# Operand parts stored by the stages, gate sums on VectorE, merge weights split in the second group

## The chip, the cores and the metric

The kernel runs on one core of a Trainium2 chip. The metric is the device time of one execution in microseconds (us), as the median of several runs. Five engines work side by side, each in the order of its own queue: TensorE (PE; its weight loads are listed as PEld), VectorE (DVE), ScalarE (ACT), GpSimd (POOL) and SyncE (SP). SP issues all transfers (DMAs) of this kernel, in the order of its queue.

## The reference

One layer over 2048 prompt rows and 8 x 16 sample rows of 1024 channels. What matters of it:

```python
h = rms_norm(x, norm_g[l])
(a_x, a_b, a_c, a_z, g_q, g_f, g_i, g_z,
 s_q, s_k, s_v, s_z, m_a, m_b, m_c) = split_cols(h @ w_in[l])
...
o_a = a_b * y_conv * jax.nn.silu(a_z)          # branch A, gated convolution
...
o_b = o_hg * jax.nn.silu(g_z)                  # branch B, linear recurrence
...
o_c = o_sb.reshape(B, T, W_SB).astype(x.dtype) * jax.nn.silu(s_z)   # branch C, stick-breaking attention
wb = w_branch[l]
y_a = o_a @ wb[:W_CONV]
y_b = o_b @ wb[W_CONV:W_CONV + W_HG]
y_c = o_c @ wb[W_CONV + W_HG:]
m = jax.nn.sigmoid(m_a) * y_a + jax.nn.sigmoid(m_b) * y_b + jax.nn.sigmoid(m_c) * y_c
return x + m @ w_out[l], conv_new, S_new.astype(x.dtype), k, v
```

All is float32. The attention is strictly causal: query block i looks at all keys before it, so later blocks cost more.

## The kernel before, in words

**Three passes per product.** A float32 operand is split into two parts (`split`, L171): ACT copies it, rounded, into the high part, and DVE subtracts that from the source to get the low part. A product is then three matmuls (`PASS3`): high x high, high x low, low x high.

**Stages.** The 17 tiles of 128 tokens are projected in three groups (`GROUPS`: 5, 6 and 6 tiles; a group has two chunks of up to 384 tokens). In a group `run_jobs` (L1241) goes through 56 channel jobs (one weight block of 128 columns, 24 matmuls per chunk, L683) and 8 token jobs (L694, two weight pieces each). After the third group comes the merge (L1321 on): four groups of 512 to 640 tokens, each with 12 branch jobs (`bjob`, three branches x by four column pieces dp) and 4 output jobs (`ojob`).

**Background work.** Between a job's pieces a planner hands out credit: the cost of each piece times a rate lets waiting background steps be recorded there. In the second group this is the attention of the sample rows; in the third group and the merge it is the prompt attention (`attn_pair`, L285), at `RATES[2]` = 0.65 and `RATE_M` = 1.0. One step of it, for 128 queries and up to 512 keys: two matmuls for the scores z (L306, L307), two sigmoids on ACT (L310, L312), a running product on DVE (L319) and a product on DVE (L324), four transposes on PE (L291), a copy aT by ACT (L292), and, after eight such steps, 16 matmuls pv with the values (L336). In the merge `bg.drain(gi)` finishes a group's attention before its branch x = 2 is loaded.

**Weights.** `wload` (L180) takes one of three buffers w (1 MB, both parts). The first time a weight is used it is loaded into a staging buffer wst (two of them, 512 KB) and split into w, and `wkeep` (L204) writes w to memory as W; later uses load W straight into w. The projection weights are split in the first group; the merge weights (12 branch pieces, 8 output pieces) in the first group of the merge. A job's weights are loaded one job ahead.

**Branch outputs.** The three branches write their outputs to OX in memory as plain float32. The merge loads them (`load_o`, L1329) through two small buffers ost, multiplies branch C by its gate SZ there, and splits each of the four row blocks into oh and ol. `bjob` multiplies the branch's product by its gate on DVE (L1374, L1376) and sums the branches with an add on POOL (L1377; on DVE only for the last branch of the last merge group). For x = 2 the sum m is split into mh and ml, some chunks late (the list `due`), for the output jobs.

**The order.** The program is recorded in the order of the Python code, and a scheduler then places each engine's instructions by its own costs and the free buffers; what it leaves is a fixed queue per engine.

## Time and profile before

| | |
|---|---|
| median of 3 runs | 2925.81 us (2923.69 to 2926.0) |
| the profiled execution, by the clock of the runs | 2919.97 us |
| its span in the trace | 2918.1 us |
| PE busy | 98% of the span, 19511 matmuls |
| DVE, ACT, POOL busy | 52%, 35%, 15% |
| DMA | 597.82 MB, 205 GB/s |

The time outside the span is 2919.97 - 2918.1 = 1.9 us. PE is busy in nearly all of the span, so time is lost or won only where PE waits; the matmuls themselves do not change. The projection of the second group runs from about 610 to 1330 us of the span, that of the third from 1350 to 2180, the merge from 2190 to the end.

### The profile page before, as it was taken

What the parts mean: (1) busy time and instruction counts of PE and PEld (TensorE: products, weight loads), DVE (VectorE), ACT (ScalarE), POOL (GpSimd) and SP (SyncE); (2) the same over time, 40 slices, a digit from 0 to 9 for tenths busy, and PEclk for the clock granted to TensorE, in tenths of its full rate; (3) what the DMA queues carried; (4) which work ended last, traced back from release to release, by engine and by line L of the source; (5) the groups of instructions that cost most, each with busy time, mean ns of one, the idle gap of its engine ahead of it and who ended that gap; (6) DMA issues with size and microseconds to landing.
All of it is one profiled execution on the core that took longest, in us unless ns stands there. A gap on an engine that the chain in (4) does not pass through costs nothing.

```text
span 2918.1 us, 51343 instructions
## 1 busy us (share of the span) xinstructions
PE 2873.3 (98%) x19511; PEld 2672.2 (92%) x19511; DVE 1530.7 (52%) x3182; ACT 1024.7 (35%) x2359; POOL 427.9 (15%) x859
## 2 busy tenths in 40 slices
PE   9999999999999999999999999999999899999999
PEld 9999999999999999999999999999988787687888
DVE  5454644641252423345434747265577876867643
ACT  4333223242222222114333443334444554444420
POOL 3200000120100000002231111101012412313210
PEclk9999999999999999999999999999999999999999
DMA  8977677767556564436764444434347776677666
GB/s 305 315 257 236 223 227 237 239 229 250 182 184 204 168 213 147 150 128 195 237 200 154 140 151 134 152 121 150 126 155 252 258 268 219 224 251 227 222 230 233
DMA packets 329224, 597.82 MB, mean 205 GB/s; under 512 B 29097, under 2 KB 231170, under 8 KB 291090
## 3 DMA queue, kind: packets, MB, share of 16 engines
q1 hardware_dynamic: 328978, 594.54, 61.8%
q8 instruction: 155, 2.54, 0.4%
q14 instruction: 91, 0.75, 0.1%
HBM read 410.62 MB, written 183.80 MB: 204 GB/s over the span
## 4 chain that ended last, share of the span: by engine, by line
PE 87%; DVE 4%; DMA 4%; issue 3%; POOL 2%; ACT 1%; SPq 0%; DVEq 0%; POOLq 0%; ACTq 0%
PE acc L683 45%; PE acc L694 13%; PE acc L1403 6%; PE acc L1368 4%; PE pv L336 4%; PE tp L291 3%; PE z L1013 2%; PE z L307 2%; PE z L306 2%; DVE pr L319 1%; PE tp L434 1%; POOL mp L1377 1%; DMA w<-W 1%; PE pv L498 1%; DMA gate<-GM 1%
## 5 line engine op out<-in xcount | busy, mean ns | idle before, releaser
L683 PE MATMUL acc<-hh,w 128*128 128x384 f32 (+1 forms) x5376 | 1465.0, 338 | 0.0
L683 PEld LDWEIGHTS acc<-hh,w 128*128 128x128 f32 x5376 | 964.3, 188 | 23.6 <-issue 17.9
L683 PE MATMUL acc<-hl,w 128*128 128x384 f32 (+1 forms) x2688 | 882.5, 328 | 0.0
L683 PEld LDWEIGHTS acc<-hl,w 128*128 128x128 f32 x2688 | 507.1, 189 | 4.9 <-issue 1.0
L694 PE MATMUL acc<-w,hh 128*128 128x256 f32 x2176 | 413.1, 286 | 1.5 <-DMA w<-W 1.2
L694 PEld LDWEIGHTS acc<-w,hh 128*128 128x128 f32 x2176 | 341.8, 188 | 4.0 <-DMA w<-W 1.5
L319 DVE TENSOR_TENSOR_SCAN pr<-snb,carry 128x513 f32<-128x513 f32 x192 | 250.6, 1306 | 117.1 <-ACT snb L310 115.6
L694 PE MATMUL acc<-w,hl 128*128 128x256 f32 x1088 | 306.8, 282 | 0.7 <-DVE hl L175 0.7
L1368 PE MATMUL acc<-oh,w 128*128 128x512 f32 (+2 forms) x960 | 295.4, 368 | 4.2 <-DMA w<-W 1.8
L292 ACT COPY aT<-tp 128x512 f32<-128x512 f32 (+2 forms) x320 | 167.6, 525 | 289.7 <-PE tp L291 289.4
L324 DVE TENSOR_TENSOR sp<-sp,pr 128x512 f32<-128x512 f32 (+2 forms) x320 | 210.3, 657 | 33.7 <-POOL sp L315 7.8
L310 ACT ACTIVATE snb<-z 128x512 f32<-128x512 f32 (+2 forms) x320 | 172.5, 539 | 129.2 <-PE z L307 120.3
L1368 PEld LDWEIGHTS acc<-oh,w 128*128 128x128 f32 x960 | 176.3, 190 | 36.9 <-DVE gate L1376 5.1
L694 PEld LDWEIGHTS acc<-w,hl 128*128 128x128 f32 x1088 | 205.1, 189 | 1.8 <-DVE hl L175 1.3
L319 DVE TENSOR_TENSOR_SCAN pr<-snb,one 128x129 f32<-128x129 f32 (+3 forms) x128 | 114.7, 896 | 163.1 <-POOL snb L315 162.9
L1403 PE MATMUL acc<-w,mh 128*128 128x256 f32 x960 | 189.1, 285 | 2.5 <-DMA w<-W 2.3
L291 PE MATMUL tp<-idf,sp 128*128 128x128 f32 x1088 | 172.0, 273 | 8.1 <-ACT aT L292 7.2
L175 DVE TENSOR_TENSOR w<-wst,w 128x1024 fp32r<-128x1024 f32 x92 | 114.9, 1249 | 121.6 <-ACT w L174 121.1
L1368 PE MATMUL acc<-ol,w 128*128 128x512 f32 (+1 forms) x480 | 174.1, 363 | 3.2 <-DVE ol L175 3.1
L312 ACT ACTIVATE sp<-z 128x512 f32<-128x512 f32 (+2 forms) x320 | 171.3, 535 | 12.6 <-DMA OX<-ot 7.5
L1403 PEld LDWEIGHTS acc<-w,mh 128*128 128x128 f32 x960 | 153.7, 188 | 10.6 <-issue 5.2
L1146 ACT ACTIVATE gm<-acc 128x384 f32<-128x384 f32 (+1 forms) x144 | 68.3, 474 | 260.8 <-PE acc L683 223.0
(296 smaller groups left out, 3730.9 us busy)
## 6 DMA issues: line engine op xcount, KB each, us to landing
w<-W SPq DMA_DIRECT2D x200, 1024.0 KB, 5.3
W<-w SPq DMA_DIRECT2D x92, 1024.0 KB, 5.0
wst<-in_w_in_dram SPq DMA_DIRECT2D x72, 512.0 KB, 6.3
GM<-gm SPq DMA_DIRECT2D x120, 192.0 KB, 2.7
Kt<-KT SPq DMA_DIRECT2D x160, 128.0 KB, 3.6
gate<-GM SPq DMA_DIRECT2D x72, 256.0 KB, 3.1
vc<-in_cache_v_dram SPq DMA_DIRECT2D x64, 256.0 KB, 3.8
kc<-in_cache_k_dram SPq DMA_DIRECT2D x64, 256.0 KB, 3.5
```

The lines of the kernel that those rows point to most:

```text
L175: return first, (eng or nc.vector).tensor_tensor(lo, src, hi.bitcast(F32), ALU.subtract)
L291: nc.tensor.transpose(tp[:, j * P:(j + 1) * P], sp[:, j * P:(j + 1) * P], idf)
L292: nc.scalar.copy(aT[:, e, 0:nb, i * P:(i + 1) * P], tp[:, :w].rearrange("p (b q) -> p b q", q=P))
L310: nc.scalar.activation(sn[:, 512 - w:512], z[:, :w], AF.Sigmoid, scale=-0.125)
L312: nc.scalar.activation(sp[:, :w], z[:, :w], AF.Sigmoid, scale=0.125)
L319: nc.vector.tensor_tensor_scan(pr[:, 512 - w:513][:, ::-1], s_in, s_in, one if diag else carry[e][i], ALU.mult, ALU.bypass)
L324: nc.vector.tensor_tensor(sp[:, :w], sp[:, :w], pr[:, 513 - w:513], ALU.mult)
L336: nc.tensor.matmul(pv[64 * e:64 * e + 64, c0:n], Vt[:, j, e], aT[:, e, j, c0:n], start=first and j == 0, stop=last and j == nb - 1, skip_g ...
L683: nc.tensor.matmul(acc[:, :n], w[0][a][:, k], hT[b][:, k, :n], start=k == 0 and i == 0, stop=k == KB - 1 and i == 2)
L694: nc.tensor.matmul(acc[:, :256], hT[b][:, k, ti * P:(ti + 1) * P], w[k // 4][a][:, k % 4], start=k == 0 and i == 0, stop=k == KB - 1 and i ...
L1368: nc.tensor.matmul(acc[:, :n], w[0][a][:, k, dd * P:(dd + 1) * P], box[x][b][:, k, sl], start=k == 0 and i == 0, stop=k == 3 and i == 2)
L1403: nc.tensor.matmul(acc[:, :256], box["l" if b else "h"][:, k, ti * P:(ti + 1) * P], w[k // 4][a][:, k % 4], start=k == 0 and i == 0, stop= ...
```

## The change

It has seven parts.

1. OX holds both parts of each branch output. The stages that make the outputs split and store them (`store_parts`): the convolution (`az`), the recurrence, the prompt attention (`store`) and the sample attention. The attention's stores also multiply by the gate SZ, which is loaded ahead.
2. `load_o` loads both parts straight into one tile o, eight DMAs and nothing else. The load for branch 0 of the next merge group is recorded ahead, in the last branch of this one; the first is recorded ahead of the first weights.
3. All sums of the branches are on DVE, and the split of m follows at once.
4. The merge weights are split and written to memory during the second group (`split_merge_weights`), one piece after the other from the ninth place on, each recorded at the second chunk of a channel job.
5. Of the loads of kept weights every fourth goes into the two wst buffers, one part each, in place of a w buffer. The last weights of the merge no longer have places of their own.
6. `RATES[2]` is 0.85 (was 0.65) and `RATE_M` 0.75 (was 1.0).
7. The two parts of the normed input, hh and hl, lie in one tile hx.

```diff
-RATES = (0.0, 0.55, 0.65)
-RATE_M = 1.0
+RATES = (0.0, 0.55, 0.85)
+RATE_M = 0.75
...
+    OX = dram.tile([3, 4, 2, P, NTOK], F32R, name="OX")
...
+    def store_parts(dst, where, x, room):
+        split(room.bitcast(F32R), x.bitcast(F32R), x)
+        for v, part in enumerate((room, x)):
+            nc.sync.dma_start(dst[v][:, where].bitcast(F32), part)
...
             if (key, n) in kept:
+                turns[0] += 1
+                if turns[0] % 4 == 0:
+                    hl = []
+                    for i in range(2):
+                        x = wp.tile([P, a, b], F32, tag="wst", name="wst", bufs=2)
+                        nc.sync.dma_start(x, kept[key, n][:, i].rearrange("p (a b) -> p a b", a=a).bitcast(F32))
+                        hl.append(x.bitcast(F32R))
+                    out.append((*hl, None))
+                    continue
+            w = wp.tile([P, 2, 1024], F32R, tag="w", name="w")
...
+            if m == m1 - 1:
+                gate.append(at.tile([P, 512], F32, tag="ot", name="ot", bufs=1))
+                nc.sync.dma_start(gate[0][:, :n], SZ[pair][:, q0:q0 + n])
...
         def store():
-            t = at.tile([P, 512], F32, tag="sp", name="ot", bufs=4)
-            nc.scalar.copy(t[:, :n], box[0][:, :n])
-            nc.sync.dma_start(OX[2, pair][:, q0:q0 + n], t[:, :n])
+            t = gate[0]
+            nc.vector.tensor_tensor(t[:, :n], box[0][:, :n], t[:, :n], ALU.mult)
+            th = at.tile([P, 512], F32, tag="oth", name="oth", bufs=1)
+            store_parts(OX[2, pair], slice(q0, q0 + n), t[:, :n], th[:, :n])
...
-            nc.sync.dma_start(OX[0, self.j][:, cols(chunk)], y)
+            store_parts(OX[0, self.j], cols(chunk), y, sg[:, :n])
...
+            oh = hs.tile([P, 2 * P], F32, tag="ktm", name="oh", bufs=1)
+            store_parts(OX[1, h], slice((first + unit[0]) * P, (first + unit[0]) * P + n), ob[:, :n], oh[:, :n])
...
+    def split_merge_weights():
+        for pieces, key in [branch_w(x, dp) for x in range(3) for dp in range(4)] + [out_w(s) for s in range(4)]:
+            for n, v in enumerate(pieces):
+                wkeep(wload([v], key, n), key, n)
+                yield
...
+        extra = split_merge_weights() if g == 1 else iter(())
         for at_, (i, ci) in enumerate(order):
+            if ci and len(jobs[i][0][0]) == 1 and at_ > 8:
+                next(extra, None)
             weights(i)
...
         def load_o(x):
-            oh = p3.tile([P, 4, GMAX], F32R, tag="oh", name="oh", bufs=2)
-            ol = p3.tile([P, 4, GMAX], F32R, tag="ol", name="ol", bufs=2)
+            o = p3.tile([P, 2, 4, GMAX], F32R, tag="o", name="o", bufs=2)
             for j in range(4):
-                st = p3.tile([P, GMAX], F32, tag="ost", name="ost", bufs=2)
-                nc.sync.dma_start(st[:, :ntok], OX[x, j][:, gcols])
-                if x == 2:
...
-                split(oh[:, j, :ntok], ol[:, j, :ntok], st[:, :ntok])
-            box[x] = (oh, ol)
+                for v in range(2):
+                    nc.sync.dma_start(o[:, v, j, :ntok].bitcast(F32), OX[x, j, v][:, gcols].bitcast(F32))
+            box[x] = (o[:, 0], o[:, 1])
...
+                if dp == 2 and x == 2 and not final:
+                    loads[gi + 1](0)
...
-                            (nc.vector if final and x == 2 else nc.gpsimd).tensor_tensor(
-                                m, m, gate[:, sl], ALU.add)
+                            nc.vector.tensor_tensor(m, m, gate[:, sl], ALU.add)
                         if x == 2:
-                            box["due"].append((box["h"][:, d, sl], box["l"][:, d, sl], m))
-                            while len(box["due"]) > (0 if final or d == 7 and chunk is pg[-1] else len(pg)):
-                                split(*box["due"].pop(0))
+                            split(box["h"][:, d, sl], box["l"][:, d, sl], m)
...
+    loads[0](0)
     ws = {0: wload(*alljobs[0][0])}
     for i, (_, compute) in enumerate(alljobs):
         if i + 1 < len(alljobs):
-            places = None
-            if i + 1 - len(alljobs) in (-3, -1):
-                places = [p3.tile([P, 4, GMAX], F32R, tag=t, name="wlast", bufs=2).rearrange("p a b -> p (a b)")
-                          [:, :2048].rearrange("p (v w) -> p v w", v=2) for t in ("oh", "ol")]
-            ws[i + 1] = wload(*alljobs[i + 1][0], places)
-        wkeep(ws[i], alljobs[i][0][1])
+            ws[i + 1] = wload(*alljobs[i + 1][0])
```

**SP's queue in the second group.** What stands in SP's queue before, at about the middle of the group's channel jobs (kc, vc and vnew are the sample attention's; w_10549 is a projection weight, loaded from its kept copy; what stands in brackets is what the row waits for, by engine or by one of eight DMA counters):

```order
L917 DMA OX_75<-y_9769 128x384 [waits DMAHW3_49,DVE_49]
L482 DMA vc_10531<-in_cache_v_dram 128x512 [waits DMAHW4_49,PE_49]
L482 DMA vc_10533<-in_cache_v_dram 128x512 [waits DMAHW5_49,PE_49]
L485 DMA vnew_6986<-VV_74 16x512 [waits DMAHW6_49,PE_49]
L1147 DMA GM_77<-gm_10348 128x384 [waits DMAHW7_49,Activation_49]
L1092 DMA OX_75<-ob_10340 128x256 [waits DMAHW0_49,DVE_49]
L189 DMA w_10549<-W31_3251 128x2048 [waits DMAHW1_49,PE_49]
```

And in the changed kernel, where two merge weight pieces are staged (wst_9683, wst_9782), written (W77, W78), and two projection weights follow (w_9743, w_9823):

```order
L211 DMA wst_9683<-in_w_branch_dram 128x4x256 [waits PE_49]
L211 DMA wst_9782<-in_w_branch_dram 128x4x256 [waits DMAHW1_49,PE_49]
L506 DMA vc_10117<-in_cache_v_dram 128x512 [waits DMAHW2_49,PE_49]
L208 DMA w_9743<-W23_2455 128x2048 [waits DMAHW3_49]
L227 DMA W77_9687<-w_9682 128x2048 [waits DMAHW4_49,DVE_49]
L227 DMA W78_9786<-w_9781 128x2048 [waits DMAHW5_49,DVE_49]
L208 DMA w_9823<-W24_2571 128x2048 [waits DMAHW6_49,DMAHW4_49]
L211 DMA wst_9902<-in_w_branch_dram 128x4x256 [waits DMAHW7_49,DMAHW0_49]
```

Before, a weight load waits for PE alone, beside the counter that it will count on itself. Now staging loads and writes stand among the weight loads: wst_9683 waits for PE, W77 for DVE, and w_9823 also for the counter DMAHW4, on which W77 counts, since it takes the buffer that W77 is written from.

**PE at the same place of the changed kernel** (acc<-hx,w is a channel job; L522 and L476 belong to the sample attention, L1040 to the recurrence; just ahead of these rows the job ends that holds wst_9630, the weight part whose buffer wst_9782 takes):

```order
L522 MATMUL pv_9715<-vc_9895,at__9889 32x128 x3
L1040 MATMUL z_9942<-WR_9931,WL_9930 128x128 [waits DVE_49,PE_49]
L476 MATMUL z_9945<-kt_9770,qz_7006 32x384 [waits PE_49]
L476 MATMUL z_9945<-kt_9770,qz_7006 32x384 x3
L1040 MATMUL z_9989<-WR_9974,WL_9973 128x128 [waits DVE_49,PE_49]
L1040 MATMUL z_10004<-WR_9993,WL_9992 128x128 [waits DVE_49,PE_49,Activation_49]
L710 MATMUL acc_9825<-hx_6801,w_9743 128x384 [waits DMAHW3_49]
L710 MATMUL acc_9825<-hx_6801,w_9743 128x384 x23
L710 MATMUL acc_9908<-hx_6980,w_9743 128x384 x24
L710 MATMUL acc_9982<-hx_6801,w_9823 128x384 [waits DMAHW6_49,Activation_49]
```

Between the last matmul of the job that frees wst_9630 and the first one with w_9823 there are now 48 matmuls with w_9743 and 31 small ones, the last ten of them shown here.

**ACT's queue in the merge.** Before, where branch C of the first merge group is loaded (snb and sp are the sigmoids of the attention):

```order
L292 COPY aT_25230<-tp_25630 128x3x128 [waits PE_49]
L310 ACTIVATE snb1_15007<-z_25646 128x512 [waits DVE_49,PE_49]
L312 ACTIVATE sp_25650<-z_25646 128x512
L174 CAST oh_25704<-ost_25706 128x640 [waits DVE_49]
L292 COPY aT_25230<-tp_25663 128x4x128 [waits PE_49]
L310 ACTIVATE snb2_15009<-z_25678 128x512 [waits PE_49,Activation_49]
L312 ACTIVATE sp_25682<-z_25678 128x512 [waits Pool_49]
L174 CAST w_25863<-wst_25864 128x1024 [waits DMAHW3_49,DMAHW0_49,PE_49]
L174 CAST oh_25704<-ost_25713 128x640 [waits DVE_49]
L292 COPY aT_25558<-tp_25758 128x4x128 [waits PE_49,Activation_49]
```

And now, in the same merge group, where the split of m begins:

```order
L311 COPY aT_26806<-tp_27057 128x4x128 [waits PE_49]
L175 CAST mh_26995<-mp_26142 128x384 [waits DMAHW4_49,DMAHW2_49,DMAHW5_49,DMAHW1_49,DMAHW6_49,DMAHW0_49,DVE_49]
L175 CAST mh_26995<-mp_26142 128x256 [waits DVE_49]
L333 ACTIVATE snb2_15328<-z_27076 128x512 [waits PE_49]
L335 ACTIVATE sp_27080<-z_27076 128x512
L175 CAST mh_26995<-mp_26142 128x384 [waits DVE_49]
L311 COPY aT_26806<-tp_27108 128x4x128 [waits PE_49]
```

The copies oh and w are gone from ACT's queue here; the copies mh, which now wait for DVE, are what is left between the attention's own instructions.

51 lines of the change are left out of this document (25 added, 26 removed).

## The prediction

> **What bounds the kernel now.** I read the stages first, then who ends PE's waits in each. The view of busy time by stretches, for the projection of the second group, that of the third, and the merge (after the length: busy us and instructions of each engine, then clock, DMA share, GB/s):
>
> ```profile
> core 0: us, PE busy (x) PEld busy (x) DVE busy (x) ACT busy (x) POOL busy (x), PEclk, DMA share, GB/s
> 610.00:1330.00 720.00, 718.33 (x5355) 698.16 (x5354) 248.49 (x728) 176.63 (x474) 42.98 (x84) 1.00 0.55 182
> 1350.00:2180.00 830.00, 828.15 (x5374) 776.32 (x5373) 459.85 (x1001) 326.99 (x817) 140.97 (x335) 1.00 0.49 157
> 2190.00:2918.00 728.00, 699.17 (x4295) 583.88 (x4295) 489.93 (x635) 299.85 (x585) 172.15 (x264) 1.00 0.72 239
> ```
>
> PE is the bound throughout. It is idle for 720 - 718.33 = 1.7 us in the second group and 1.9 us in the third: nothing is to be won there, only to be lost. The merge has 728 - 699.17 = 28.8 us of idle PE. What ended PE's waits in the merge, first on the matmuls, then on the weight loads, which wait earlier and so count more (us in total, times, longest):
>
> ```profile
> PE pv L336 <- ACT aT L292: 7.5, 5, 2.7
> PE tp L291 <- ACT aT L292: 7.2, 6, 3.3
> PE acc L1368 <- DVE ol L175: 3.1, 2, 1.9
> PE z L306 <- ACT sp L312: 2.4, 4, 1.4
> PE acc L1368 <- ACT oh L174: 1.6, 2, 1.5
> ```
>
> ```profile
> PEld pv L336 <- ACT aT L292: 13.2, 8, 3.6
> PEld tp L291 <- ACT aT L292: 9.0, 6, 3.5
> PEld acc L1368 <- DVE gate L1376: 5.1, 7, 2.0
> PEld acc L1368 <- DVE ol L175: 4.9, 4, 2.3
> PEld z L306 <- ACT sp L312: 3.6, 4, 1.6
> PEld acc L1368 <- ACT oh L174: 3.2, 3, 1.9
> PEld acc L1403 <- DVE pr L319: 1.8, 1, 1.8
> ```
>
> ACT is the one that is late, and yet it is busy for 300 of 728 us. It stands still with work behind it. Three rows of the timeline in the merge show how (start, length, in brackets the idle time ahead):
>
> ```profile
> 2479.67 0.62 ACT L174 CAST oh<-ost 128x512 fp32r<-128x512 f32 x1 [7.44 <-DVE ost L1338]
> 2480.20 0.58 ACT L292 COPY aT<-tp 128x512 f32<-128x512 f32 x1
> 2683.26 0.62 ACT L174 CAST mh<-mp 128x512 fp32r<-128x512 f32 x1 [4.17 <-POOL mp L1377]
> ```
>
> The copy oh heads ACT's queue and waits 7.44 us for a loaded and multiplied branch output. The attention's copy aT is behind it and PE behind that. At 2683 the same is done by mh, which waits for POOL's add.
>
> **The change, part by part.** *The merge.* The loads of both parts take oh, its DVE half ol and the product with SZ out of the merge, and weight splits too; POOL's adds go to DVE. So the waits for aT and sp lose their cause, in all 7.5 + 7.2 + 2.4 = 17.1 us by the matmuls, 13.2 + 9.0 + 3.6 = 25.8 us by the weight loads. The copies mh stay and now wait for DVE; they fall in one branch of three, so I leave 5 us of waits: of the middle, 21.5, I count 16 as won. The waits for oh and ol (4.7 to 8.1 us) go as well, but the first load of the merge takes their place. It reads 8 x 320 KB = 2.6 MB, and its buffers come free only when the projection's do, some 4 us of PE work (as the order of PE has it) ahead of the first branch matmul. The nearest rows are the load of one part before and the highest rates of the merge's slices:
>
> ```profile
> ost<-OX SPq DMA_DIRECT2D x12, 320.0 KB, 4.3
> GB/s 230 267 309 271 219 276 230 238 300 211 287 252 219 242 233 218 261 215 214 220 242 234 260 228 202 302 184 234 250 223 224 187 238 195 205 295 321 325 220 73
> ```
>
> At 309 to 325 GB/s it takes some 8.3 us and the first landing adds about 1; the last row block is needed 5.5 us after the issue (4, and 9 matmuls). That is a stall of about 4 us where 6.4 stood (the middle of 4.7 and 8.1): -2. Later loads have 14 us or more of PE work ahead of them and are hidden; without that cover each would cost this much again. DVE's own late rows (gate 5.1, pr 1.8) I take to improve by 2, with DVE's load: it loses 48 ol (41.9 us), 17 weight splits (23.1), 16 products (11.6) and the attention that moves out, and gains POOL's 72 adds, at the length of the 8 that DVE made already:
>
> ```profile
> L175 DVE TENSOR_TENSOR ol<-ost,oh 128x512 fp32r<-128x512 f32 (+1 forms) x48 | 41.9, 877 | 13.7 <-ACT oh L174 13.6
> L175 DVE TENSOR_TENSOR w<-wst,w 128x1024 fp32r<-128x1024 f32 x17 | 23.1, 1359 | 7.1 <-ACT w L174 7.1
> L1338 DVE TENSOR_TENSOR ost<-ost,szt 128x512 f32<-128x512 f32 (+1 forms) x16 | 11.6, 726 | 26.4 <-DMA szt<-SZ 26.3
> L1377 DVE TENSOR_TENSOR mp<-mp,gate 128x512 f32<-128x512 f32 x8 | 6.0, 755 | 0.2
> ```
>
> ```profile
> L1377 POOL TENSOR_TENSOR mp<-mp,gate 128x512 f32<-128x512 f32 (+1 forms) x72 | 108.3, 1508 | 144.7 <-DVE gate L1376 132.0 <-issue 12.2 <-DMA gate<-GM 0.3
> ```
>
> The adds cost 72 x 0.755 = 54 us on DVE against 76.6 removed; hidden, as long as DVE stays under PE. Sum for the merge -16 - 2 - 2 = **-20**; ends: -33 (25.8 and 8.1 and 5.1 all gone, 4 and 2 kept) and -12 (17.1, of which 5 stay, and no other gain).
>
> *The second group, where the merge weights are now split.* In each pair a staging buffer comes free when a job ends, wst is loaded, ACT and DVE split it, W is written, and only the landing of that write frees the buffer of a following projection weight, which is then loaded. SP issues in order, so the other weight loads of that place stand behind the waiting W too. The rows for this chain (loads and writes: KB, median us to landing; first the whole run, then the merge, then the second group):
>
> ```profile
> W<-w SPq DMA_DIRECT2D x92, 1024.0 KB, 5.0
> ```
>
> ```profile
> w<-W SPq DMA_DIRECT2D x56, 1024.0 KB, 6.2
> W<-w SPq DMA_DIRECT2D x18, 1024.0 KB, 5.9
> wst<-in_w_branch_dram SPq DMA_DIRECT2D x9, 512.0 KB, 6.4
> wst<-in_w_out_dram SPq DMA_DIRECT2D x8, 512.0 KB, 7.3
> ```
>
> ```profile
> w<-W SPq DMA_DIRECT2D x57, 1024.0 KB, 5.5
> xt<-in_x_prompt_dram SPq DMA_DIRECT2D x1, 512.0 KB, 4.8
> ```
>
> ```profile
> L174 ACT CAST w<-wst 128x1024 fp32r<-128x1024 f32 x17 | 17.9, 1054 | 13.2 <-DMA wst<-in_w_branch_dram 9.1 <-DMA Vt<-VV 2.5 <-PE acc L1403 1.3
> ```
>
> From the release to the landed weight: 6.4 + 1.05 + 1.36 + 5.0 + 5.5 = 19.3 us; with the merge's landings 6.4 + 2.4 + 5.9 + 6.2 = 20.9; I take 19.6, nearer the first, whose rows come from more transfers and from this group. The PE work that covers it, at the place shown in the order: 48 matmuls of 384 columns and 31 small ones, by these rows of the chain of waits:
>
> ```profile
> 816.12 4.22 PE acc L683 x24
> ```
>
> ```profile
> 2121.17 0.22 PE z L1013 x2
> ```
>
> 2 x 4.22 + 31 x 0.11 + 0.3 (four are longer) = 12.1 us. So PE stands 19.6 - 12.1 = 7.5 us there, part of them already at w_9743, which stands in SP's queue behind the staging loads. I count five such places in the new order: the covers are 14.2, 12.1, 14.3, 12.2 and 13.0 us, 65.8 together. 5 x 19.6 - 66 = 32; at a sixth place a weight load stands behind one staging load and is late by about 1 (issue 1.8 us after the release, 5.5 to landing, against 6.9 us of cover: 0.4, and SP's issues between); PE's own small gaps lengthen the covers by some 4%, -3. **+30.** Ends: 5 x (4.8 + 2.4 + 5.0 + 5.5) - 66 = 22 and 5 x (7.3 + 2.4 + 5.9 + 6.2) - 66 = 43.
>
> [...]
>
> *The third group.* Of the 320 running products of the attention 164 stand ahead of the first merge gate in DVE's order before, 210 now. The 46 more bring their products along, and the branches' splits add about 20 us:
>
> ```profile
> L324 DVE TENSOR_TENSOR sp<-sp,pr 128x512 f32<-128x512 f32 (+3 forms) x158 | 91.9, 581 | 14.6 <-POOL sp L315 2.8 <-DVE sc L1014 0.3
> L319 DVE TENSOR_TENSOR_SCAN pr<-snb,carry 128x513 f32<-128x513 f32 x71 | 91.3, 1285 | 77.2 <-ACT snb L310 76.2
> L319 DVE TENSOR_TENSOR_SCAN pr<-snb,one 128x129 f32<-128x129 f32 (+1 forms) x88 | 79.0, 897 | 136.9 <-POOL snb L315 136.7
> ```
>
> 46 x (1.1 + 0.58) = 77 us; DVE goes from 460 of 830 (55%) to 557 of some 875 (64%). In the merge, at 490 of 728 (67%), rows ended by DVE other than ol cost PE 5.1 + 1.8 = 6.9 us. **+6**; ends 0 (nothing waited at 55%) and 16, if the recurrence's chain of short DVE steps waits twice as often.
>
> *The rest, at nothing:* the outputs' splits and second stores run 14 us or more ahead of their use, behind PE; the stores' longer chain of DVE, ACT, DVE and DMA (about 2 us by the rows of 512 columns above, and a landing) would show only if the attention finished late, and its last store stands 40 us of PE work ahead of its matmuls. SP issues 200 DMAs more in 2900 us. The last weights keep 9 us of PE work ahead of them.
>
> **Sum** -20 + 30 + 6 = +16 for the profiled execution: 2920 + 16 = 2936. The median shown is 2925.8 - 2920.0 = 5.8 higher than that execution, so the forecast is **2942**. With all terms at their low ends it is -33 + 22 + 0 = -11, 2915; with all at their high ends -12 + 43 + 16 = +47, 2973.
>
> **Rivals.** (1) *The merge gains more than the second group loses*: one mechanism, ACT's queue without the waiting copies. For it speaks that ACT works only 300 of 728 us; against it the copies mh that stay. It decides where the gain passes 28 us with the loss at its low end, 22: -33 + 22 + 2 = -9, 2917; a little beyond these ends, 2910. (2) *The two cancel*: the short chain (22) with a gain of 24 and the third group at 2: 2926. For it: PE waits by weight loads are the larger count. (3) *DVE becomes the bound in the third group*: the recurrence's bursts already fill 40 of 50 us here, and the added 11% of load make that 46 or more:
>
> ```profile
> 1600.00:1650.00 50.00, 50.00 (x315) 46.55 (x315) 39.73 (x107) 20.17 (x54) 8.12 (x24) 1.00 0.38 127
> ```
>
> Five such bursts at 4 to 5 us each would be +22 in place of +6: 2958. That the planner does not move the attention is ruled out by the counts 164 and 210.
>
> **How the numbers follow.** My forecast, slower by 7 to 26 us (2933 to 2952), 0.50; rival 3, 0.12; rival 2, 0.18; rival 1, 0.20. What a measurement can tell from no change is about 0.2%, 5.9 us. Faster is rival 1, 0.20; same is rival 2, 0.18; slower is the forecast and rival 3, 0.62. The range reaches down into rival 1, to 2911, and up over rival 3 to 2967; about one in ten lies outside at either end.
>
> **What would show it.** Right: in the second group PE waits of 2 to 8 us that end by DMA w<-W, in five places, some 30 us in all, with SP waiting for the split ahead of W; in the merge hardly a wait for aT, and PE idle of about 10 us; one wait of some 4 us for o<-OX at its start. Wrong: w<-W waits below 15 us in the second group, or waits for aT that stay because mh waits for DVE, or PE waits for DVE in the third group above 15 us.

## The result, and the profile after

The changed kernel takes **2944.76 us** (median of 5, 2940.6 to 2947.1), the kernel before 2924.93 us in the same session. The ratio is 1.0067, with a 95% interval of 1.0055 to 1.0080: slower by 0.7%. The forecast was 2942.

First the busy time by stretches, with the borders at the same projection matmuls (the 3900th and the 7200th) and at the first matmul of the merge in both kernels, so that each row holds one stage. Before:

```profile
core 0: us, PE busy (x) PEld busy (x) DVE busy (x) ACT busy (x) POOL busy (x), PEclk, DMA share, GB/s
636.80:1273.00 636.20, 635.72 (x4776) 616.85 (x4775) 205.60 (x595) 159.58 (x421) 32.51 (x65) 1.00 0.57 187
1273.00:2187.70 914.70, 909.17 (x5876) 852.84 (x5874) 510.94 (x1138) 354.71 (x886) 147.74 (x354) 1.00 0.49 158
2187.70:2918.10 730.40, 700.39 (x4300) 584.65 (x4300) 492.09 (x637) 302.15 (x589) 172.15 (x264) 1.00 0.72 238
```

After:

```profile
637.70:1326.40 688.70, 656.55 (x4777) 627.19 (x4776) 234.31 (x632) 183.53 (x456) 32.71 (x65) 0.98 0.66 223
1326.40:2308.60 982.20, 969.26 (x6214) 892.16 (x6213) 606.07 (x1275) 425.57 (x1045) 166.24 (x416) 1.00 0.51 164
2308.60:2940.90 632.30, 628.76 (x3962) 540.99 (x3962) 373.95 (x545) 196.84 (x387) 39.61 (x131) 1.00 0.80 266
```

The second group has the same PE work (4776 and 4777 matmuls) and takes 688.7 us where it took 636.2: **+52.5**. The third group and the merge must be read together, since attention moved from the one to the other: 1614.5 where 1645.1 stood, **-30.6**. Before the second group both kernels are within 1 us. That is the 22.8 us by which the spans differ (2940.9 and 2918.1). So both terms have the sign that was forecast, and both are far larger: +52.5 for +30, and -30.6 for -20 + 6 = -14. Two errors of some 20 us each cancelled in the total: that it came out at 2944.8 for 2942 is luck.

**The second group after.** What ended PE's waits there (us in total, times, longest):

```profile
PE acc L710 <- DMA w<-W: 9.0, 3, 4.1
PE z L1040 <- DVE WL L1035: 6.3, 2, 5.5
PE hg L827 <- DVE kt L176: 5.5, 4, 3.9
PE tp L458 <- ACT kt L459: 2.9, 3, 2.4
PE tp L458 <- DMA kc<-in_cache_k_dram: 2.4, 2, 2.2
PE tp L499 <- DVE sps L490: 1.0, 1, 1.0
```

The prediction had named weight loads, with some 30 us, and called itself wrong below 15. They end 9.0 us. The larger part, 6.3 + 5.5 + 2.9 + 1.0 = 15.7 us, ends with ACT and DVE. The timeline shows what held them. ACT and PE at 725, then SP and PE at 956 to 965:

```profile
725.18 1.04 ACT L175 CAST w<-wst 128x1024 fp32r<-128x1024 f32 x1 [2.10 <-DMA wst<-in_w_branch_dram]
726.88 1.08 ACT L459 COPY kt<-tp 128x512 f32<-128x512 f32 x2
727.52 0.66 PE L458 MATMUL tp<-idf,kc 128*128 128x128 f32 x4 [2.43 <-ACT kt L459]
```

```profile
956.26 0.93 SPq L211 DMA_DIRECT2D wst<-in_w_out_dram  x2
957.24 0.49 SPq L529 DMA_DIRECT2D OCS<-od  x1
957.78 0.41 SPq L208 DMA_DIRECT2D w<-W  x1
```

```profile
964.89 1.33 PE L710 MATMUL acc<-hx,w 128*128 128x384 f32 x3 [4.09 <-DMA w<-W]
```

At 725 the split of a merge weight heads ACT's queue until its staging load has landed; kt, for which PE waits, is behind it. That is the picture which the change removed from the merge, now in another stage. It is not the whole of it. At 853, the longest wait (5.5 us, for WL), DVE stands still for 1.2 us and works for 2.4 us on two splits that stand one behind the other, ahead of the recurrence. At 764 (3.9 us, for the kt of L176) a split was also waiting, but the buffer of kt was itself held until two stores QT<-kt had landed, at 765.5 and 765.8, so that the split can account for about 1 us there.

PE's own order is part of it too. In the second group of the changed kernel there are six places where 43 to 74 matmuls of the sample attention, the recurrence and the key transposes follow one another without one of a projection job; they last 4.6 to 11.9 us each, and some 20 of PE's 32 us of waits lie inside them. In the kernel before, the longest such stretch of the stage is 45 matmuls, 1.8 us, without a wait. These small matmuls wait for ACT and DVE step by step, so PE has nothing else to do while it waits. At 957 the weight load stands in SP's queue behind two staging loads, as the prediction had it for the first weights; the write W is issued only at 963, behind it.

**The granted clock fell too.** By stretches of 50 us in the second group:

```profile
700.00:750.00 50.00, 46.53 (x369) 43.34 (x368) 6.68 (x11) 12.25 (x28) 2.40 (x4) 0.97 0.65 217
750.00:800.00 50.00, 44.47 (x350) 42.09 (x349) 17.51 (x40) 14.04 (x37) 11.74 (x20) 0.93 0.71 233
850.00:900.00 50.00, 44.37 (x319) 42.66 (x318) 31.17 (x94) 13.41 (x31) 1.32 (x4) 0.93 0.77 270
950.00:1000.00 50.00, 42.62 (x282) 39.47 (x281) 8.54 (x10) 13.11 (x25) 0.00 (x0) 0.93 0.85 297
1000.00:1050.00 50.00, 43.88 (x312) 41.30 (x311) 22.33 (x61) 16.15 (x41) 0.81 (x4) 0.93 0.78 286
```

These five rows lose (0.03 + 4 x 0.07) x 50 = 15.5 us to the clock; the other rows of the stage show 1.00. With the added idle time, (688.70 - 656.55) - (636.20 - 635.72) = 31.7 us, that is 47 of the 52.5 us. The last 5 lie in what the view counts as PE's busy time, and no run shows what they are. So the idle time came out as forecast (30), and the clock was left out.

**The merge after.** PE's waits in it are nearly gone, and yet ACT still waits for sums before it copies mh. All of PE's waits of the changed merge, then ACT's largest that do not end with PE, of the merge before and after:

```profile
PE acc L1402 <- DMA o<-OX: 0.6, 1, 0.6
PE acc L1402 <- DVE mp L1408: 0.2, 1, 0.2
```

```profile
ACT mh L174 <- POOL mp L1377: 58.1, 28, 5.6
ACT mh L174 <- DVE mp L1377: 45.0, 8, 27.0
ACT oh L174 <- DVE ost L1338: 40.2, 12, 7.4
ACT oh L174 <- DMA ost<-OX: 23.8, 11, 4.0
ACT w L174 <- DMA wst<-in_w_branch_dram: 9.1, 4, 4.8
```

```profile
ACT mh L175 <- DVE mp L1411: 110.3, 36, 47.9
```

A wait of 110 us for DVE's sums costs PE next to nothing here (0.8 us of waits in all). The size of an off-path engine's wait does not tell its price; which of the rows before were paid for had to be found by runs.

### The profile page after: what moved, and what is told of

Its sections match the earlier page's. It is cut to its first block, busy times and chain, and to the rows that moved or that the text cites. A ratio compares the mean times of both kernels' runs of the same rounds, so it can differ in the third digit from the quotient of the medians.

```text
span 2940.9 us, 51568 instructions
## 1 busy us (share of the span) xinstructions
PE 2883.8 (98%) x19511; PEld 2678.8 (91%) x19511; DVE 1542.1 (52%) x3284; ACT 1021.3 (35%) x2371; POOL 315.4 (11%) x787
## 4 chain that ended last, share of the span: by engine, by line
PE 71%; DVE 5%; DMA 2%; issue 1%; POOL 1%; ACT 1%; SPq 0%; DVEq 0%; POOLq 0%; ACTq 0%
PE acc L710 29%; PE acc L1402 10%; PE acc L721 8%; PE acc L1433 7%; PE pv L359 4%; PE tp L310 4%; PE z L329 2%; PE z L330 2%; DVE pr L342 1%; PE z L1040 1%; PE tp L458 1%; DVE sp L347 1%; POOL rr L234 1%; PE pv L522 1%; DMA wst<-in_w_branch_dram 0%
## 5 line engine op out<-in xcount | busy, mean ns | idle before, releaser
L710 PE MATMUL acc<-hx,w 128*128 128x384 f32 (+1 forms) x6816 | 1262.9, 334 | 9.1 <-DMA w<-W 9.0
L710 PEld LDWEIGHTS acc<-hx,w 128*128 128x128 f32 x6816 | 1116.3, 190 | 32.2 <-issue 15.6
L721 PE MATMUL acc<-w,hx 128*128 128x256 f32 x2544 | 328.1, 284 | 1.8 <-DVE hx L176 0.8
L721 PEld LDWEIGHTS acc<-w,hx 128*128 128x128 f32 x2544 | 311.6, 188 | 5.0 <-DVE hx L176 1.6
L710 PE MATMUL acc<-hx,wst 128*128 128x384 f32 x1248 | 250.1, 344 | 1.0 <-DVE hgz L1134 0.8
L1402 PE MATMUL acc<-o,w 128*128 128x512 f32 (+2 forms) x1080 | 231.6, 363 | 0.8 <-DMA o<-OX 0.6
L710 PEld LDWEIGHTS acc<-hx,wst 128*128 128x128 f32 x1248 | 215.4, 188 | 11.2 <-issue 6.1
L176 DVE TENSOR_TENSOR w<-wst,w 128x1024 fp32r<-128x1024 f32 x92 | 112.5, 1223 | 196.9 <-ACT w L175 190.3
L1402 PEld LDWEIGHTS acc<-o,w 128*128 128x128 f32 x1080 | 184.7, 188 | 32.1 <-issue 2.6
L347 DVE TENSOR_TENSOR sp<-sp,pr 128x512 f32<-128x512 f32 (+2 forms) x320 | 195.6, 612 | 25.1
L310 PEld LDWEIGHTS tp<-idf,sp 128*128 128x128 f32 x1088 | 132.4, 141 | 15.2 <-issue 3.4
L329 PE MATMUL z<-Kt,Q 128*128 128x512 f32 (+2 forms) x320 | 128.6, 402 | 1.2 <-DVE sc L1041 0.6
```

Of the source, the lines that this page charges most:

```text
L310: nc.tensor.transpose(tp[:, j * P:(j + 1) * P], sp[:, j * P:(j + 1) * P], idf)
L329: nc.tensor.matmul(z[:, :w], Q1[:, i * P:(i + 1) * P], Kt[:, :w], start=True, stop=False)
L347: nc.vector.tensor_tensor(sp[:, :w], sp[:, :w], pr[:, 513 - w:513], ALU.mult)
L710: nc.tensor.matmul(acc[:, :n], w[0][a][:, k], hT[b][:, k, :n], start=k == 0 and i == 0, stop=k == KB - 1 and i == 2)
L721: nc.tensor.matmul(acc[:, :256], hT[b][:, k, ti * P:(ti + 1) * P], w[k // 4][a][:, k % 4], start=k == 0 and i == 0, stop=k == KB - 1 and i ...
L1402: nc.tensor.matmul(acc[:, :n], w[0][a][:, k, dd * P:(dd + 1) * P], box[x][b][:, k, sl], start=k == 0 and i == 0, stop=k == 3 and i == 2)
```

## Experiments

The rows by stage below are counted as above. Each run's time stands beside a run of the kernel before on the same chip: 2925.35 us for the first four, 2926.07 for e6 to e9, 2926.53 for e10 to e12, 2923.77 for e13. These agree within 3 us, and runs of different sessions are compared on that footing.

### The second group: what makes it wait

**e4, splits behind the turn's loads.** The split is recorded after the loads of the turn's own weights:

```diff
-            if ci and len(jobs[i][0][0]) == 1 and at_ > 8:
-                next(extra, None)
             weights(i)
             if g or at_:
                 weights(i + 1)
+            if ci and len(jobs[i][0][0]) == 1 and at_ > 8:
+                next(extra, None)
```

> The changed kernel, with each split of a merge weight recorded behind the loads of the turn's own projection weights instead of ahead of them, so that SP issues these loads first. Theory Q: ACT and DVE still wait for the staging load with work behind them: 2930 to 2945, and PE waits ended by ACT and DVE stay at some 16 us. Theory S: the weight loads no longer stand behind the staging loads and the writes: the waits ended by weight loads (9.0 us by the matmuls) and the half clock after them (6.8 us lost) mostly go, and with them some of the rest: 2915 to 2928.

Measured: 2942.85 us (2938.1 to 2944.2). The instructions of all five engines stand in the same order as in the changed kernel: the scheduler undid the edit. So the run tells the theories apart in nothing. It is the changed kernel once more, and shows that its time comes back within 2 us.

**e5, splits on POOL.**

```diff
-                    split(hi, lo, st)
+                    if pool:
+                        nc.gpsimd.tensor_copy(hi, st)
+                        nc.gpsimd.tensor_tensor(lo, st, hi.bitcast(F32), ALU.subtract)
+                    else:
+                        split(hi, lo, st)
...
-                wkeep(wload([v], key, n), key, n)
+                wkeep(wload([v], key, n, True), key, n)
```

> The changed kernel, with the twenty splits of merge weights done on POOL (a copy and a subtraction there) instead of ACT and DVE; loads, writes and their order in the program are the same. POOL's adds of 128x512 took 1.5 us before, so a split of 128x1024 takes it some 5 to 6 us where ACT and DVE take 2.4. Theory Q: no wait of PE ends by ACT or DVE behind a split, some 16 us of waits and 8.5 us of half clock less, but the chain of loads gets longer by 3 us a piece: 2917 to 2935. Theory S: the longer chain costs 3 us more at five places and more half clock: 2955 to 2970.

Measured: 2962.1 us, in the range of theory S, but not for its reason. PE's longest wait, 7.0 us at 856, ends with DVE's WL as in the changed kernel. POOL, then DVE, in that place:

```profile
855.04 2.47 POOL L219 TENSOR_TENSOR w<-wst,w 128x1024 fp32r<-128x1024 f32 x1
```

```profile
855.03 0.28 DVE L1039 TENSOR_TENSOR WL<-hgk,X 128x128 f32<-128x128 f32 x1
855.35 2.31 DVE L1040 TENSOR_TENSOR X<-X,hgf 128x128 f32<-128x128 f32 x1
857.59 1.78 DVE L493 TENSOR_TENSOR_SCAN pr<-sns,pr 128x385 f32<-128x385 f32 x1
859.29 2.36 DVE L1041 TENSOR_TENSOR hgf<-hgf 128x128 f32<-128x128 f32 x1
```

Of the 26 products of 128x128 on DVE from 845 to 866 the two at 855.35 and 859.29 take 2.31 and 2.36 us, beside POOL's two subtractions (855.04 to 857.51 and 858.64 to 861.50); one beside POOL's copy, at 854.19, takes 0.92, the other 23 take 0.28 to 0.32. So the edit brought a cost of its own, and does not decide between Q and S. It does show that the wait for kt at 764 is in the main not the split's: with the split on POOL it is still 3.1 us long, and ACT's copy waits for the store:

```profile
767.48 0.37 ACT L175 CAST kt<-hg 128x256 fp32r<-128x256 f32 x1 [1.48 <-DMA QT<-kt]
```

**e6, the waits alone.** To the kernel of e1 (below) the loads and splits are added, without writes and in a buffer of their own:

```diff
+                st = xq.tile([P, a, b], F32, tag="mst", name="mst", bufs=1)
+                nc.sync.dma_start(st, v)
+                split(st.bitcast(F32R), st.bitcast(F32R), st)
+                yield
```

> The kernel of e1_split_in_merge (2921.5 us: all of the change but the moved splits), with the disputed cost by itself added at the same twenty turns of the second group: each loads a 512 KB piece into a buffer of its own and splits it in place on ACT and DVE as the changed kernel does, but writes nothing to memory and takes no projection weight's buffer, so no chain of loads hangs on it. The result of that splitting is not used; the merge splits its weights itself. Theory Q (heads of ACT's and DVE's queues that wait for a staging load cost 28 of the 52.6 us, or more): 2921 + 25 to 45 = 2946 to 2966. Theory S (the chain through SP's queue and the weight buffers is the cost): 2921 to 2928, the splits' own 2.4 us being hidden.

Measured: 2927.3 us, 5.9 more than e1. Theory S is not borne out by it, because the splits did not stay where they were written (engine, count, shortest/median/longest in ns, first and last start in us):

```profile
L175 ACT CAST mst<-mst x20: 1043/1048/1062, 131.2 to 321.0; 128x1024 fp32r<-128x1024 f32 x20
```

With a buffer that nothing else uses, the scheduler drew all twenty into the first group. The run says only that twenty such splits cost some 6 us there; on theories Q and S it says nothing.

**e10, splits without the write.** The splits stay in the weight and staging buffers, which hold them in their place; the write to memory is left out, and the merge splits its weights itself, as in e1:

```diff
-                wkeep(wload([v], key, n), key, n)
+                wload([v], key, n)
...
             ws[i + 1] = wload(*alljobs[i + 1][0])
+        wkeep(ws[i], alljobs[i][0][1])
```

> The changed kernel with the same twenty loads and splits at the same turns of the second group, through the same staging and weight buffers, but the parts are not written to memory; the merge loads and splits its weights itself, as in e1_split_in_merge (2921.5), which is the base to compare with. The waits of ACT and DVE for the staging load stay as they were; the chain of the prediction loses its write of 5.0 us, and SP no longer stands at the write until the split is done. Theory Q (queue heads of ACT and DVE): the second group still loses 28 us or more: 2946 to 2965. Theory S (the chain): 5 x (19.6 - 5.0) = 73 against 66 of cover, 7 us left: 2924 to 2932.

Measured: 2973.1 us, 51.6 above its base e1 (2921.5). Its second group (684.1 us against 635.3 in e1: 48.8 more):

```profile
635.80:1319.90 684.10, 657.47 (x4775) 630.08 (x4774) 234.93 (x632) 184.07 (x456) 32.77 (x65) 0.97 0.58 194
```

Its waits are those of the changed kernel: DVE kt 5.0, DVE WL 4.5, ACT kt 3.3, and 6.0 for w<-W. Without the write's 5.0 us in the chain theory S had 7 us left; nearly all of the loss is still there. The chain through W is not the cause. PE's order has the same six stretches of small matmuls as in the changed kernel, so the run leaves them together with the waits of ACT and DVE.

**e3, staged a turn ahead.** Each piece is loaded into a buffer of its own right after the split of the one before it, and split at the next turn:

```diff
+            st = xq.tile([P, a, b], F32, tag="mst", name="mst", bufs=1)
+            nc.sync.dma_start(st, v)
...
+            split(hi, lo, st)
+            wkeep([(hi, lo, w)], key, n)
+            if at_ + 1 < len(todo):
+                st = stage(todo[at_ + 1][0])
+            yield
```

> The changed kernel, with the merge weights still split in the second group, but each piece's staging load has a buffer of its own and is issued a whole turn (14 us of PE work or more) ahead of its split, so that neither ACT nor SP waits for it. Theory Q: the 16 us of PE waits behind the splits on ACT and DVE and the half clock after them (five windows of 3.4 us, 8.5 us lost) go, and the rest of the second group's loss, some 25 us, stays or shrinks: 2900 to 2922. Theory S: the chain loses its first link, 6.4 of 19.6 us, at five places whose covers are 12 to 14 us: nearly the whole loss goes: 2893 to 2900. If neither holds and traffic is the cause (the same bytes move): 2935 to 2945.

Measured: **2901.2 us**, ratio to the kernel before 0.9917 (0.9901 to 0.9932): 43.6 us below the changed kernel. The splits still run at 692 to 987 us, the same bytes move (152 MB in the stage, at 237 GB/s), and the writes W are made. The copies of the splits on ACT in the second group, with ACT's idle time ahead of them and what ended it, in the changed kernel and here:

```profile
L175 ACT CAST w<-wst 128x1024 fp32r<-128x1024 f32 x20 | 21.0, 1049 | 26.8 <-DMA wst<-in_w_branch_dram 13.2 <-PE acc L710 7.9 <-DMA wst<-in_w_out_dram 5.7
```

```profile
L175 ACT CAST w<-mst 128x1024 fp32r<-128x1024 f32 x20 | 21.0, 1048 | 11.8 <-DMA mst<-in_w_branch_dram 7.3 <-DMA mst<-in_w_out_dram 3.8 <-PE acc L710 0.7
```

The second group takes 645.2 us: 9 of the 52.5 are left.

```profile
635.80:1281.00 645.20, 641.71 (x4776) 615.32 (x4775) 235.88 (x632) 184.44 (x456) 32.98 (x65) 1.00 0.69 237
```

No weight load is among its rows of PE's waits, the row z <- WL falls from 6.3 to 0.5, and the clock is 1.00. So the staging load, issued where its split is needed and into buffers that PE still reads, was the cause of 43 us. By which way is less clear. ACT's waits ahead of the splits fall from 26.8 to 11.8 us, but those for the staging loads among them only from 18.9 to 11.1, and DVE's waits for ACT's half only from 80.9 to 68.7. What goes altogether are the six stretches of small matmuls: the longest without a projection job is again 45 matmuls and 1.8 us, so that PE has other work while ACT and DVE wait. Three things thus change with this one edit: the heads of ACT's and DVE's queues, the weight loads behind the staging loads in SP's queue, and PE's order. No run takes them apart, and the edit gives the load a buffer as well as time; which of these two does more was not tried.

### The merge: what its gain comes from

**e1, splits in the merge again.**

```diff
-        extra = split_merge_weights() if g == 1 else iter(())
+        extra = iter(())
...
             ws[i + 1] = wload(*alljobs[i + 1][0])
+        wkeep(ws[i], alljobs[i][0][1])
```

> The changed kernel, with the twenty merge weight pieces split in the merge again, where the kernel before split them, and all else as changed. It tells how much the moved splits cost. The second group then is as before: its 52.6 us of loss should be gone. Theory Q (in the second group the splits stand at the head of ACT's and DVE's queues until their staging load lands, and PE waits for what is behind them; in the merge the same splits do the same): 2944.8 - 52.6 = 2892, and about 10 us of new waits in the merge, since ACT waited 13.2 us for staging loads there before: 2895 to 2908. Theory S (the loss is the chain of weight loads behind SP's queue; in the merge few loads follow a split, and nothing is lost): 2890 to 2897. Rival M (the merge's gain came mainly from the splits that left it, not from the branch outputs' parts): 2915 to 2926.

Measured: 2921.5 us, ratio 0.9989 (0.9979 to 0.9998): rival M's range. The second group is back at 635.3 us, and the merge takes 666.8 where the changed kernel took 632.3, so the move is worth 34.5 us in the merge and costs 53.4 in the second group. That seemed to say that the splits by themselves had made the merge wait. The next runs say otherwise.

**e7, the moved splits alone.** The kernel before, with the splits moved and staged as in e3, and nothing else of the change.

```diff
+            if ci and len(jobs[i][0][0]) == 1 and at_ > 8:
+                next(extra, None)
             weights(i)
```

> The kernel before with only the splits of the merge weights moved to the second group, each piece staged a turn ahead in a buffer of its own as in e3_stage_a_turn_ahead (2901.2); branch outputs, additions, rates and kept loads as before. Theory W (the weight splits alone made the merge's waits): the merge gains the 34.5 us that lie between e1 and the changed kernel, the second group loses the 9.9 us of e3: 2925 - 34.5 + 9.9 = 2901, as e3. Theory O (the copies oh that wait for the branch outputs hold ACT's queue just the same, as the prediction had it; both causes must go): the waits for aT stay, 2918 to 2930. Mixed: 2905 to 2917.

Measured: 2934.0 us, above every range. The second group pays 11.9 us (648.1), and the merge gains nothing: 731.8 us against 730.4, with 17.6 us of PE waits for aT. Theory W falls.

**e9, POOL's additions back in e3.**

```diff
-                            nc.vector.tensor_tensor(m, m, gate[:, sl], ALU.add)
+                            (nc.vector if final and x == 2 else nc.gpsimd).tensor_tensor(
+                                m, m, gate[:, sl], ALU.add)
                         if x == 2:
-                            split(box["h"][:, d, sl], box["l"][:, d, sl], m)
+                            box["due"].append((box["h"][:, d, sl], box["l"][:, d, sl], m))
+                            while len(box["due"]) > (0 if final or d == 7 and chunk is pg[-1] else len(pg)):
+                                split(*box["due"].pop(0))
```

> The kernel of e3_stage_a_turn_ahead with the merge's additions on POOL and the delayed splits of their sums, as before the change. If POOL's 1.5 us additions hold up the copies mh on ACT, and the attention's copies behind them, as in the row of the prediction (4.17 us once), in one branch of three: 2904 to 2912. If POOL's instructions also slow DVE's that run beside them (in the run with the splits on POOL a 128x128 product on DVE took 2.31 us beside one of them, 0.29 elsewhere), some 5 us more of it can show: up to 2916. If neither reaches PE: 2898 to 2903.

Measured: 2921.6 us, 20.4 above e3 and above every range. The merge takes 655.9 us against 633.7, and PE waits 8.2 us for aT in two waits, of which the longest is 5.0. The additions weigh far more than I had given them.

**e13, the additions alone.** The reverse edit of e9, on the kernel before:

```diff
-                            (nc.vector if final and x == 2 else nc.gpsimd).tensor_tensor(
-                                m, m, gate[:, sl], ALU.add)
+                            nc.vector.tensor_tensor(m, m, gate[:, sl], ALU.add)
                         if x == 2:
-                            box["due"].append((box["h"][:, d, sl], box["l"][:, d, sl], m))
-                            while len(box["due"]) > (0 if final or d == 7 and chunk is pg[-1] else len(pg)):
-                                split(*box["due"].pop(0))
+                            split(box["h"][:, d, sl], box["l"][:, d, sl], m)
```

> The kernel before with one thing changed: the merge's additions on VectorE, and each sum split as soon as it is made. Weight splits, branch outputs, rates and loads are as before. ACT waited 58.1 us for POOL's additions in the merge before, more than for any other cause. If these waits are the ones that reach PE: the whole of what e9 against e3 (20.4 us) or e11 against e7 (31.5 us) showed, 2895 to 2907. If the weight splits, which keep ACT waiting 13.2 us for their loads, take the place (as e1 with all but the moved splits gained only 4 us): 2918 to 2928. Between: 2908 to 2917, and the three causes add up in part.

Measured: **2895.9 us**, ratio 0.9894 (0.9873 to 0.9914). That is the first expectation. This one part of the change makes the kernel faster by 28 us. Its merge by stretches, and PE's largest waits in it:

```profile
2189.10:2898.40 709.30, 694.39 (x4300) 582.22 (x4300) 497.36 (x709) 302.60 (x589) 65.26 (x192) 1.00 0.74 246
```

```profile
PE tp L291 <- ACT aT L292: 3.8, 1, 3.8
PE acc L1367 <- DVE ol L175: 2.1, 2, 1.9
PE acc L1367 <- ACT oh L174: 2.0, 2, 1.6
```

The merge is 21 us shorter (709.3 for 730.4; the profiled execution was the slowest of the four, and that of the kernel before lies 5.8 us below its median, hence 21 and not 28), and the waits for aT fall from 14.7 us to 4.4, though the copies oh and the weight splits are all still there. Three things change at once with the additions: mh no longer waits for POOL (58.1 us before), the sums are split as soon as they are made, and DVE no longer runs beside POOL's additions. The first is smaller than it looks, since the copies mh now wait for DVE, 85.5 us where that row had 45.0:

```profile
ACT mh L174 <- DVE mp L1376: 85.5, 33, 25.0
```

In all ACT stands still for 103.1 us ahead of mh before and for 85.5 here. The same DVE product before and in e13, in the merge:

```profile
L324 DVE TENSOR_TENSOR sp<-sp,pr 128x512 f32<-128x512 f32 x130 | 103.1, 794 | 12.1 <-ACT aT L292 0.5 <-ACT oh L174 0.5
```

```profile
L324 DVE TENSOR_TENSOR sp<-sp,pr 128x512 f32<-128x512 f32 x131 | 90.1, 688 | 9.9
```

It takes 688 ns instead of 794, which agrees with e5. DVE's busy time in the merge hardly moves (497 for 492) with 72 additions more. How much of the 21 us comes from the order of the waits and how much from the faster DVE was not separated.

**e11, staged splits and additions, without the parts.** The kernel of e7 with the additions on DVE:

```diff
-                            (nc.vector if final and x == 2 else nc.gpsimd).tensor_tensor(
-                                m, m, gate[:, sl], ALU.add)
+                            nc.vector.tensor_tensor(m, m, gate[:, sl], ALU.add)
```

> The kernel of e8_staged_old_rates (2892.4) without the branch outputs' parts: outputs are stored whole, and the merge loads, multiplies and splits them itself as before; moved and staged weight splits, the additions on VectorE and the old rates stay. It is the kernel before with two things changed. If each of the three (splits, POOL's additions, outputs' copies) holds ACT's queue by itself, and the merge gains only when the last is gone: 2915 to 2930. If the additions on VectorE were the missing one, and the parts do little: 2892 to 2902. The prediction gave the parts the largest share, 16 of 20 us: 2906 to 2914 would answer to that.

Measured: 2902.5 us, 31.5 below e7: the additions again, and at the upper end of the range for parts that do little. It lies 10.1 above e8, but e8 has the kept halves as well as the parts. e12 below has the parts without the halves and takes 2907.1, 4.6 more than this run. So with splits and additions moved, the parts of the branch outputs by themselves gain nothing, though the prediction had credited them and the splits with all of the waits for aT; the merge takes 697.1 us here and 696.6 in e12.

In the order e13, e11, e12, e8 the 39.2 us that the merge gains at the old rates (730.4 to 691.2, e8 below) are 21.1 for the additions, 12.2 for the moved splits, 0.5 for the parts and what else e12 has of the change, and 5.4 for the kept halves. In another order the shares are others: without the additions the moved splits gain nothing (e7). And what the moved splits win here they cost in the second group, which takes 648.7 us in e11 and 636.4 in e13: as a whole e11 is 6.6 us slower than e13. Of the 39.2 us 25.1 are idle time of PE (730.40 - 700.39 = 30.0 before, 691.20 - 686.28 = 4.9 in e8); the other 14 lie in what the view counts as busy, and no run shows what they are.

**What stays open in e1.** e13 has the weight splits in the merge and 2895.9 us. e1 has the splits there too, the additions on DVE and the parts, and 2921.5. The two differ also in the rates (9 us, below), in the kept halves that go through the staging buffers, which the merge's splits use as well, and in the place of the last weights. ACT's waits for staging loads in e1's merge are longer than in e13's, 13.1 + 9.5 us (longest 7.5) against 9.1 (longest 4.7), and so the shared staging buffers are a candidate. But PE's own waits in e1's merge end with DVE, 6.6 us for sp in six waits and 4.1 for yt, and its clock there is 0.99, some 7 of its 666.8 us. No run takes these apart.

### Rates and kept halves

**e8, e3 with the old rates.**

```diff
-RATES = (0.0, 0.55, 0.85)
-RATE_M = 0.75
+RATES = (0.0, 0.55, 0.65)
+RATE_M = 1.0
```

> The kernel of e3_stage_a_turn_ahead with the two rates as before (0.65 and 1.0 in place of 0.85 and 0.75), so that about 46 of the attention's steps go back from the third group to the merge. If the attention is only moved, and PE is the bound on both sides: 2898 to 2906. If the merge needs the lower density of attention to keep ACT and DVE ahead of PE: 2908 to 2920, with waits for aT and sp back in the merge. If the third group paid for it with its DVE (the +6 of the prediction): 2892 to 2897.

Measured: **2892.4 us**, ratio 0.9887 (0.9870 to 0.9904), the fastest of all, in the range of the third expectation, 8.8 below e3 and 52 below the changed kernel. It is only 3.5 us below e13, and the intervals of the two ratios overlap: nearly all that the change can gain comes from the additions. With the attention where it was before, the stages compare directly with the kernel before:

```profile
636.60:1281.90 645.30, 641.37 (x4776) 615.45 (x4775) 235.81 (x632) 184.40 (x456) 33.17 (x65) 1.00 0.70 237
1281.90:2198.40 916.50, 909.98 (x5883) 853.73 (x5881) 534.09 (x1184) 365.35 (x913) 149.64 (x354) 1.00 0.52 168
2198.40:2889.60 691.20, 686.28 (x4294) 580.18 (x4294) 448.66 (x636) 258.70 (x518) 57.59 (x192) 1.00 0.77 254
```

+9.1 in the second group, +1.8 in the third, -39.2 in the merge.

**e12, e8 with every kept weight loaded whole.**

```diff
-                if turns[0] % 4 == 0:
+                if False:
```

> The kernel of e8_staged_old_rates (2892.4) with every kept weight loaded whole into its own buffer, as before the change, in place of every fourth one in two halves into the staging buffers. If the halves spare the weight buffers in which the moved splits stand, and so cover the landing of their writes (12.9 us of chain now, 12 to 14 of cover): 2900 to 2912, with waits ended by weight loads in the second group. If the chain is short enough without them: 2888 to 2896.

Measured: 2907.1 us, 14.7 above e8, within the range of the first expectation. The second group takes 655.5 us for 645.3. But its waits are 4.7 us for the sample's keys and only 2.2 for a weight load, so the halves help there by a way that was not the one expected.

## Why the prediction was right, and where it was not

The number and the sign were right (2942 for 2944.8), within the forecast's own 2933 to 2952, but by two errors that cancelled: the loss was 22 us larger than forecast and the rest 17 us better. By its terms:

- **Second group, +30, ends 22 and 43: measured +52.5, outside.** The idle time came out (31.7 us), but mostly by another mechanism, so that its size is luck. The chain "release, load, split, write, load" is not what PE waited for: e10 leaves out the write and keeps 48.8 us. What failed is the step that let the split only lengthen a chain of loads; I had not asked what stands behind it in ACT's and DVE's queues, though that was my own reading of the merge. With it failed the cover: the 31 small matmuls were counted as 0.11 us of PE work each, but they wait for ACT and DVE themselves, and the stretch at 848 lasted 11.9 us. These queues end 15.7 us of PE's waits, weight loads 9.0. By the prediction's own test, "w<-W waits below 15 us", this step was wrong. The part on the first weights behind SP's staging loads is seen at 957.
- **The clock, not in the sum: about 15.5 us.** Around the wait at 853 the five-microsecond stretches show it:

```profile
850.00:855.00 5.00, 3.03 (x38) 1.64 (x36) 3.64 (x13) 2.31 (x4) 0.00 (x0) 1.00 1.02 351
855.00:860.00 5.00, 1.33 (x5) 1.37 (x6) 4.93 (x15) 0.76 (x2) 0.00 (x0) 0.57 0.99 415
860.00:865.00 5.00, 5.00 (x24) 5.00 (x23) 1.34 (x5) 0.32 (x1) 0.22 (x1) 0.75 0.90 328
865.00:870.00 5.00, 5.00 (x30) 5.00 (x29) 0.00 (x0) 1.13 (x3) 0.00 (x0) 1.00 0.66 226
```

  (0.43 + 0.25) x 5 = 3.4 us lost behind one wait of 5.5 us: the granted clock is 0.50 from 855.7 to 862.5, 6.8 us. The kernel before has such a stretch too, behind the longest of PE's waits: 3.25 us for aT at 2683, then 3.4 us at 0.50 from 2687.3. As an estimate from these two, with half of each stretch lost, the term would have been five places times 1.7 to 3.4 us, 9 to 17.
- **Merge, -20, ends -33 and -12: measured -39.2 where it can be read alone (e8), outside.** The step that failed is "the copies mh stay and now wait for DVE; ... I leave 5 us of waits", with the additions counted only as DVE's hidden work. The additions alone give 21 of the 39 us (e13). With the splits moved as well the merge takes 697 (e11), with the kept halves 691 (e8); the parts, which with the splits were credited with all the waits for aT, change it by 0.5 (e11 against e12). Among ACT's own waits before, POOL's sums are the largest row that does not end with PE, 58.1 us; the prediction had them as one example, 4.17 us. The low end of -33 was also more than PE's whole idle time in the merge, 28.8 us; the measured gain is too, and 14 us of it came out of PE's busy time, which the prediction and the text ahead of it ("only where PE waits") did not expect.
- **Third group and rates, +6, ends 0 and 16: measured +8.6** (-30.6 for the two stages, less the -39.2), and 8.8 by e3 against e8. Right in size. PE's idle time in the third group is 12.9 us for 5.5 before, spread over rows of at most 3.8 us (DVE's Sn, 1.3 before); with the old rates it is 6.5 (e8).
- **The first load of the merge, a stall of 4: measured 0.6** (o<-OX). Too high. The 1 us in it for the first landing was an estimate for which the prediction shows no row.
- Of the rivals, (3) did not occur: DVE's rows in the third group stay below 4 us each. Rival (1), the merge's gain above the second group's loss, would have decided from 28 us on. The gain passed that, but the loss was not at its low end. With the staging load a turn ahead it is the outcome (e3, e8). Rival (2), the two cancel, needed the loss at 22.

## What to carry to other kernels

A load, a split of it and a store that are moved to a stage "with room" need room at the heads of the queues, not only in busy time: issue the load a turn of work ahead of the first instruction that must wait for it (43 of 52 us came back that way). Look also at what PE's own order holds in that place: here some 20 of PE's 32 us of waits lay inside the stretches of small matmuls, which wait for ACT and DVE step by step and which the prediction had counted as cover. When several late producers stand in one queue, the size of their waits does not tell which is paid for: in the changed merge ACT waits 110.3 us for sums and PE 0.8 us in all. Try the edits singly: here one part of the change made the kernel 28 us faster by itself, and a bundle with all but one of its parts gained 4. Count with a new PE wait what the clock takes after it: in the traces of the kernels before and after PE waits 3.0 us or more five times (3.25 at 2683 before; 3.89, 5.46, 4.09 and 3.02 at 764, 853, 961 and 1015 after), and each time a stretch at a granted clock of 0.50, of 3.4 or 6.8 us, begins before the wait has ended or within 1 us behind it. Counted at half its length, such a stretch costs 1.7 or 3.4 us.

## What was not expected of the hardware

- DVE was slower beside POOL: 128x128 products, elsewhere of 0.28 to 0.32 us, took 2.31 and 2.36 us while POOL subtracted 128x1024 (e5), and the mean of a 128x512 product fell from 794 to 688 ns when POOL's additions went (e13).
- The half clock also followed some waits shorter than 3 us: around 725 us, where the waits were 2.4 us (tp <- kt) and 1.0 us (tp <- sps) one behind the other, the row of 700 to 750 shows 0.97 (0.50 from 729.4 to 732.8). A wait of 1.9 us at 975 was followed by it too (0.50 from 978.6 to 982.0), one of 2.7 us at 2546 in the kernel before was not (1.00 from 2540 to 2560).
- The 1 MB weight loads landed in 5.9 us at the median of the changed second group, at 223 GB/s, against 5.4 at 187 before: 0.5 us more beside 36 GB/s more traffic. In e3 they took 6.1 us at 237 GB/s, and no wait of PE in the stage was longer than 0.8 us.
